# A gated delta rule in two halves of the tokens with all heads, and one attention pipeline over all head pairs

## The chip, the cores and the metric

The kernel runs on one core of a Trainium2 chip. The metric is the time of one execution on the device in microseconds; lower is better. The kernel before took 1449.81 us in the median of three runs (1449.51 to 1454.9).

## The reference

One transformer block in fp32: 1024 tokens, width 1024. The input is normalised and modulated by a condition vector (`mod`, six vectors of width 1024 from the product `silu(c) @ w_ada`), then projected. The projection feeds an attention with eight heads of 64 and a gated delta rule with eight heads of 64. Their outputs, side by side, pass an output projection `w_out`; a gated feed-forward network and a last normalisation follow.

```
proj = h @ w_in                      # q_a k_a v_a | q_d k_d v_d z_d | b_d a_d
y_attn  = dilated_attention(q_a, k_a, v_a, rel_bias)
qkv     = silu(causal_conv(q_d | k_d | v_d, width 4 along the tokens))
q, k    = l2norm per head;  beta = sigmoid(b_d);  g = -exp(a_log) * softplus(a_d + dt_bias)
# delta rule in chunks: within a chunk a unit lower triangular system is solved, then
for chunk in chunks:                 # one after the other, for each head
    v_new = u - w @ state
    o     = (q * exp(g)) @ state + qk @ v_new
    state = state * exp(g_last) + k_dec.T @ v_new
y_delta = rmsnorm(o) * silu(z_d)
x = x + g1 * (concat(y_attn, y_delta) @ w_out)
x = x + g2 * ((silu(h2 @ w_gate) * (h2 @ w_up)) @ w_down);  out = rmsnorm(x)
```

The outputs of a chunk depend on all earlier chunks of the same head through `state` alone; heads do not depend on each other.

## The kernel before

Engines are named as in the profile: PE (TensorE), DVE (VectorE), ACT (ScalarE), POOL (GpSimd), SP (which issues the DMAs). The kernel is one long program for a scheduler that puts the instructions into the queue of each engine. It follows program order as priority, by its own idea of when an operand is ready; an instruction that stands later in the program is moved ahead where it thinks an engine would be free. On the chip each engine works its queue in order.

**Products.** The large projections are done in two-part precision: each fp32 operand is split into a high and a low part, and three matmuls take the place of one. The split of the weights is `wsplit` (L209): a slab of 128 x 512 is loaded (256 KB, three buffers), cast on ACT (L215) and subtracted on POOL (L216), with five buffers for each part. The normalised input lies split in SBUF as `hh` and `hl`, eight tiles each.

**First stage (to about 113 us).** The first four column blocks (`first`: k and q of the delta heads 0 to 3) and two v blocks (L478, both halves of the tokens) are multiplied while the input is still being split (`normed`, `split`, L436 to L458). Two q blocks follow for the second token half (L602).

**Fill.** All other projections stand in a generator, `others` (L1103), that yields after every few matmuls with a nominal cost (0.64 us for three matmuls of 512 columns, 0.32 for three of 256). `proj_d` (L571) multiplies one block of 128 columns for both halves of the tokens with the same two slabs (10.24 nominal us); `proj_t` (L579) makes one block of 256 columns for all eight token blocks with four slabs (20.48). The order is: z of group 0; k, q and v of group 1; z of group 1; v of the attention (`va`, two blocks); q and k of the attention for the four head pairs. Results go to DRAM through `spill`. `mixed` (L1123) adds the modulation products (`mods`, L1081: a 256 KB load `wm` and eight small matmuls at a time). Fill is drawn at given points: `turn(name)` draws what `FILL[name]` says ahead of the product of that name and pins the product behind it, `until` draws until a part is done, and `hold(*LEVELS[g])` (L1136) draws until a part is done and then a stated number of nominal us, and pins the first step of the inverse behind it. FILL has 25 entries, `"trv3_0": 10.24` and `"S0_0_0": 14.08` the largest.

**Delta rule (about 95 to 482 us).** `delta(g)` (L1163) runs once for each of two groups of four heads, over all 1024 tokens: convolution (`conv`, L529), transposes (`delta_turn`, L705), decays and products within the chunk of 128 tokens (`delta_prep`, L730, kk at L776), v (`delta_v`, L821, transposes trv at L833), the inverse (`delta_inverse`, L843: 31 steps of substitution on DVE in blocks of 32, L862 and L866, a trip through DRAM, then the blocks joined per head) and the scan (`delta_scan`, L945). The scan takes the eight chunks in turn, each with two head pairs. A step of `state` (L946) is: two products with the state (L957), four operations R (L962), four products (L971), two copies, two products (L979) and four updates of the state S (L990). `readout` (L996) makes the output of the step before, `flip` (L1030) transposes it (yt, L1035) and stores it in DRAM. After the first scan `delta_early` (L1152) prepares q and k of group 1.

**Attention (482 to 711 us).** A unit is one head pair and one block of 128 queries: scores S (L1252, L1253), softmax, transposes tr (L1276, named et in FILL) and the product with the values y (L1293), pipelined over units in `attend` (L1308), the transposes one unit behind and the value products three behind:

```
    attend(range(EARLY))          # EARLY = 1: the eight units of pair 0
    run(fill[0])                  # all projections that are left
    sh_.close()                   # hh and hl are given up; yh, yl take their place
    ...                           # the delta rule's output is loaded (y_load)
    fill[0] = out_delta()         # half of the output projection is the new fill
    attend(range(EARLY, 4))       # the 24 units of pairs 1 to 3
```

`att_load` (L1205) loads q and k of a pair, head by head, into `raw` (two buffers) and converts them (QS, KS on ACT and DVE, KL on POOL). After this the rest of the output projection and the feed-forward network follow, which the change does not touch.

## Time and profile before

| | us |
|---|---|
| median of 3 runs | 1449.81 |
| lowest, highest run | 1449.51, 1454.9 |
| the profiled execution | 1446.69 |
| its span on the core | 1445.0 |
| mean granted clock of PE in it | 0.981 |

The span runs from the first to the last instruction; the execution's time has 1.7 us more around it. In the profile a group or a piece is named by line, engine, operation and output <- inputs, with shapes as partitions x elements and x for the number of instructions. A matmul's end is modelled, so that neighbouring matmuls overlap in the listing and a busy PE is not PE at its peak. The granted clock is a share of full speed.

### The profile page before, as it was taken

The numbers are of one execution on the slowest core, as the hardware profiler recorded it, in microseconds if no ns is written. First come the engines' busy times: TensorE is split into PE (matmuls) and PEld (weight loads), VectorE is DVE, ScalarE is ACT, GpSimd is POOL, SyncE is SP. The second block draws the span as 40 slices with busy tenths as digits, with TensorE's granted clock in tenths as the row PEclk, the third lists the DMA queues.
The fourth block names the chain that finished last, engine by engine and source line by source line (L and its number), as shares of the span: only waits on it lengthen the run. The fifth ranks groups of instructions, "written<-read, shape, count | busy, mean of one in ns | idle before, by whom it ended". The sixth has DMA issues, their size and how long they took to land.

```text
span 1445.0 us, 24561 instructions
## 1 busy us (share of the span) xinstructions
PE 1379.9 (95%) x8984; PEld 1119.5 (77%) x8984; DVE 873.4 (60%) x1660; ACT 670.0 (46%) x1283; POOL 305.2 (21%) x279
## 2 busy tenths in 40 slices
PE   7998989997999979999999989999999999999997
PEld 4777857786888758777877868888888888888885
DVE  3687762665736241366426997757676676475487
ACT  3487523348233263576437743333333333444456
POOL 1345412243323343444245310000000000000000
PEclk9998999998999989999999999999999999999999
DMA  8736464466532526642275445636354565866676
GB/s 304 246 114 175 136 200 144 147 191 178 158 95 63 172 68 182 189 132 92 81 237 167 154 138 173 206 111 210 125 178 144 167 211 182 268 213 206 191 222 236
DMA packets 171921, 245.69 MB, mean 170 GB/s; under 512 B 33078, under 2 KB 76391, under 8 KB 171800
## 3 DMA queue, kind: packets, MB, share of 16 engines
q1 hardware_dynamic: 171800, 244.12, 53.4%
q8 instruction: 71, 1.16, 0.3%
q14 instruction: 50, 0.41, 0.1%
HBM read 181.30 MB, written 67.48 MB: 172 GB/s over the span
## 4 chain that ended last, share of the span: by engine, by line
PE 62%; DVE 6%; DMA 5%; ACT 3%; issue 2%; POOL 1%; SPq 0%; DVEq 0%; ACTq 0%; POOLq 0%
PE wua L1525 8%; PE wga L1525 8%; PE X L1720 6%; PE g_a L567 5%; PE wuc L1525 4%; PE Z L1720 4%; PE wgc L1525 4%; PE g_va L590 4%; PE wo L567 2%; PE y L1293 2%; PE tr L1276 2%; PE Y L1720 2%; PE wgb L1525 2%; PE wub L1525 2%; PE S L1252 1%
## 5 line engine op out<-in xcount | busy, mean ns | idle before, releaser
L1515 DVE TENSOR_TENSOR wl_db<-wr_db,wh_db 128x512 fp32r<-128x512 f32 x77 | 53.2, 690 | 76.1 <-ACT wh_db L1514 75.9
L1514 ACT CAST wh_db<-wr_db 128x512 fp32r<-128x512 f32 x77 | 47.9, 622 | 98.3 <-PE X L1720 41.3
L1720 PE MATMUL X<-wl_db,wh_da 128*128 128x512 f32 x176 | 68.6, 390 | 0.2 <-DVE wl_db L1515 0.2
L1720 PE MATMUL X<-wh_db,wl_da 128*128 128x512 f32 x176 | 68.5, 389 | 0.0
L1720 PE MATMUL X<-wh_db,wh_da 128*128 128x512 f32 x176 | 68.5, 389 | 0.0
L1263 POOL TENSOR_SCALAR X<-X,sc 128x128 f32<-128x128 f32 (+7 forms) x64 | 47.8, 751 | 69.6 <-DVE sc L1262 57.2
L1261 ACT ACTIVATE X<-X,sc 128x128 f32<-128x128 f32 (+7 forms) x64 | 49.6, 776 | 22.8 <-DVE sc L1256 17.3
L1256 DVE CUSTOM_DVE_ANT_0 X<-S,ng 128x512 f32<-128x512 f32 (+3 forms) x64 | 36.9, 586 | 34.8 <-PE S L1253 25.8
L1515 DVE TENSOR_TENSOR wl_da<-wr_da,wh_da 128x512 fp32r<-128x512 f32 x77 | 52.7, 685 | 1.2 <-ACT wh_da L1514 1.2
L567 PE MATMUL wo<-yh,wh_wo 128*128 128x512 f32 x128 | 52.0, 408 | 0.7 <-ACT yh L1359 0.4
L567 PE MATMUL g_a<-hh,wh_a 128*128 128x512 f32 x128 | 51.4, 401 | 0.0
L567 PE MATMUL g_a<-hl,wh_a 128*128 128x512 f32 x128 | 51.1, 399 | 0.0
L567 PE MATMUL g_a<-hh,wl_a 128*128 128x512 f32 x128 | 51.0, 398 | 0.0
L567 PE MATMUL wo<-yl,wh_wo 128*128 128x512 f32 x128 | 50.6, 396 | 0.0
L567 PE MATMUL wo<-yh,wl_wo 128*128 128x512 f32 x128 | 50.5, 395 | 0.0
L1514 ACT CAST wh_da<-wr_da 128x512 fp32r<-128x512 f32 x77 | 47.3, 616 | 5.9 <-PE wua L1525 5.8
L1222 DVE SCALAR_TENSOR_TENSOR QS<-raw,QS 64x1024 fp32r<-64x1024 f32 x8 | 12.6, 1572 | 61.7 <-ACT QS L1221 61.6
L1276 PE MATMUL tr<-ident,X 128*128 128x128 f32 x288 | 45.2, 283 | 1.6 <-ACT et L1281 1.2
L1514 ACT CAST wh_wg_s<-wg_s 128x512 fp32r<-128x512 f32 x33 | 20.5, 622 | 55.4 <-PE wuc L1525 23.8
L1293 PE MATMUL y<-et,va 128*64 128x128 f32 x576 | 45.9, 285 | 0.0
L1252 PE MATMUL S<-KS,QS 128*128 128x512 f32 (+3 forms) x96 | 36.9, 394 | 7.3 <-ACT KS L1226 4.9
L216 POOL TENSOR_TENSOR wl_wo<-wr_wo,wh_wo 128x512 fp32r<-128x512 f32 x24 | 32.0, 1337 | 50.8 <-ACT wh_wo L215 40.7
(545 smaller groups left out, 4397.9 us busy)
## 6 DMA issues: line engine op xcount, KB each, us to landing
wr_da<-ao_d SPq DMA_DIRECT2D x77, 256.0 KB, 3.3
wm<-in_wada SPq DMA_DIRECT2D x64, 256.0 KB, 3.7
wr_wu<-in_wu SPq DMA_DIRECT2D x50, 256.0 KB, 2.8
wr_wg<-in_wg SPq DMA_DIRECT2D x48, 256.0 KB, 3.1
ao_d<-a SPq DMA_DIRECT2D x44, 256.0 KB, 2.6
wr_wd<-in_wdn SPq DMA_DIRECT2D x44, 256.0 KB, 3.1
wr_db<-wt_d SPq DMA_DIRECT2D x44, 256.0 KB, 2.9
ao_d<-as SPq DMA_DIRECT2D x33, 256.0 KB, 2.0
```

The lines of the kernel that those rows point to most:

```text
L567: last[0] = nc.tensor.matmul(ps, a[:, w0], b[k0 + k4][:, cs], start=(i == 0), stop=(i == n - 1))
L590: last[0] = nc.tensor.matmul(ps[:, :n], a[k][:, ts_], b[:, w0], start=(i == 0), stop=(i == 23))
L1252: nc.tensor.matmul(ps[:, 0 : c1 - c0], QS[:, qs], KS[:, c0:c1], start=True, stop=False)
L1256: nc.vector.tensor_tensor_reduce(out=X[:, c0:c1], in0=ps[:, 0 : c1 - c0], in1=ng[:, u + c0 : u + c1], scale=1.0, scalar=(3e38 if m is None ...
L1261: nc.scalar.activation(X[:, 0:nk], X[:, 0:nk], AF.Exp, scale=-1.0, bias=m, accum_out=sc[:, 2:3])
L1263: nc.gpsimd.tensor_scalar(out=X[:, 0:nk], in0=X[:, 0:nk], scalar1=sc[:, 3:4], scalar2=0.0, op0=ALU.mult, op1=ALU.add)
L1276: nc.tensor.transpose(ps[:, (kb - c0) * P : (kb - c0 + 1) * P], X[:, kb * P : kb * P + P], ident)
L1293: nc.tensor.matmul(yps[64 * e : 64 * e + 64, yc], va[:, kb, 64 * e : 64 * e + 64], ets[e][:, kb, :], start=(kb == 0), stop=(kb == qb),)
L1514: nc.scalar.copy(hi, src)
L1515: (eng or nc.vector).tensor_tensor(out=lo, in0=src, in1=hi.bitcast(F32), op=ALU.subtract)
L1525: nc.tensor.matmul(ps, a[:, w0], b, start=(first and k == 0 and n_ == 0), stop=(k == 3 and n_ == 2), skip_group_check=True,)
L1720: nc.tensor.matmul(bank[b], a[:, ts_], w, start=(first and f == 0 and n_ == 0), stop=(f == NF - 1 and n_ == 2), skip_group_check=True,)
```

## The change

The delta rule is cut the other way: `delta(g)` now runs over one half of the tokens (four chunks) for all eight heads, and the second run goes on from the state of the first. The scan has two times four steps with four head pairs each; the readout handles 512 columns at once.

- First stage: the four blocks of `first` are now k of all eight heads; the two blocks beside the input's split are q of pairs 0 and 1, for the first half of the tokens only; q of pairs 2 and 3 follows, first half only. v comes wholly from the fill, through DRAM.
- Fill: k, q, v and z are projected one half of the tokens at a time (`proj_h`, and `proj_t` over four token blocks), each time with slabs loaded anew. The order is v (first half), z (first half), k, q, v, z (second half), then va 0, pair 0, va 1, pair 1, pair 2, pair 3.
- Convolutions, transposes, norms and v are done on tiles of two pairs x 512 tokens. A convolution of the second half needs the last tokens of the first; they are kept as four columns ahead of it in DRAM.
- `LU`, the number of buffers of the tag that holds decays, v and the inverse, goes from 5 to 6. Small constants and the states move from one pool to another.
- `LEVELS` and `FILL` change: eight entries of FILL go, all of them for the delta rule.
- Attention: one pipeline over all 32 units. The fill that is left is dealt out evenly over the first 14 units (`FRONT` is the nominal sum of all fill), and the change of pools (`switch`) happens inside the pipeline, ahead of the value product of pair 1's fourth block. `raw` has four buffers instead of two.

```diff
-LEVELS = ("qd", 4), ("z1", 36)
+LU = 6
+LEVELS = (("qd", 1), 0), (("vd", 1), 24)
+FRONT = 4 * 20.48 + 4 * 5.12 + 5 * 10.24 + 8 * 10.24
...
-    "trv3_0": 10.24,
...
-    V0 = 16
+    V0 = 8
...
+    def proj_h(col, hf, name, evac):
+
+        slabs = [(wsplit(I["wd"][col, s], 512, f"{name}_{s}"), 4 * s) for s in range(2)]
+        ps = gbank(f"g_{name}")
+        yield from gemm(ps, slabs, hh, hl, slice(hf * HALF, (hf + 1) * HALF))
+        evac(hf, ps)
...
-        yield from proj_t(I["wz0"], 256, "z0", z_evac(0))
-        yield from group1(("kd", "qd", "vd"))
-        yield from proj_t(I["wz1"], 256, "z1", z_evac(1))
-        done.add("z1")
-        for c in range(2):
-            yield from proj_t(I["wva"][c], 256, f"va{c}", va_end(c))
-        done.add("va")
+        yield from half_of("vd", VD, range(4), 0)
+        for g in range(2):
+            yield from proj_t((I["wz0"], I["wz1"])[g], 256, f"z{g}_0", z_evac(g), range(4))
+        done.add(("z", 0))
+        yield from half_of("kd", KD, range(2, 4), 1)
+        yield from half_of("qd", QD, range(4), 1)
+        yield from half_of("vd", VD, range(4), 1)
+        for g in range(2):
+            yield from proj_t((I["wz0"], I["wz1"])[g], 256, f"z{g}_1", z_evac(g), range(4, 8))
+        done.add(("z", 1))
         for hp in range(4):
+            if hp < 2:
+                yield from proj_t(I["wva"][hp], 256, f"va{hp}", va_end(hp))
+                done.add(f"va{hp}")
...
             for Q in range(2):
+                with turn(f"sb{g}_{n}_{Q}"):
+                    for q in (2 * Q, 2 * Q + 1):
...
-        for n in range(8 + 3):
-            if n < 8:
+        for n in range(4 + 2):
+            if n < 4:
                 state(n)
...
-                r = pa.tile([P, T], F32, name=f"raw{kk}_{h}", tag="raw", bufs=2)
+                r = pa.tile([P, T], F32, name=f"raw{kk}_{h}", tag="raw", bufs=4)
...
-    def attend(hps):
-        units = [(hp, qb) for hp in hps for qb in range(TB)]
+    def attend(switch):
+        units = [(hp, qb) for hp in range(4) for qb in range(TB)]
         xs, ets = {}, {}
         for i in range(len(units) + AV):
+            if i >= AV and units[i - AV] == (EARLY, 3):
+                switch()
             if i < len(units):
                 hp, qb = units[i]
                 if hp not in loaded:
+                    until(lambda: hp in done)
                     loaded[hp] = att_load(hp)
-                if qb == 2 and hp < 3 and hp + 1 in done:
+                if i < EARLY * TB + 3 + AV:
+                    ahead((FRONT - used[0]) / (EARLY * TB + 3 + AV - i))
+                if qb >= 2 and hp < 3 and hp + 1 in done and hp + 1 not in loaded:
                     loaded[hp + 1] = att_load(hp + 1)
...
-    attend(range(EARLY))
-    run(fill[0])
-    sh_.close()
...
-    fill[0] = out_delta()
-    attend(range(EARLY, 4))
+    attend(switch)
```

More of the change, by code (lines that the diff above doesn't have):

```diff
@@ L482, in build @@
         for k in range(KT):
-            step(k, range(2))
+            if hf == 0:
+                step(k, range(2))
             split(k, hf)
@@ L800, in delta_prep @@
+        for q in range(4):
             with tc.issue_after(sel[g].ins):
@@ L953, in state @@
[L953 to L961 removed]
+            So = [S[q][N % 3] for q in range(4)]
+            Sn = [S[q][(N + 1) % 3] for q in range(4)]
@@ L1138, in hold @@
         until(lambda: what in done)
-        while us > 0:
-            us -= next(fill[0])
+        ahead(us)
         return tc.issue_after(last[0].ins)
@@ L1144, in until, with fetch @@
         while not ready():
-            next(fill[0])
-    def fetch(i, name):
-        xp = pd.tile([P, T], F32, name=f"xp_{name}", tag="xp", bufs=2)
-        nc.sync.dma_start(xp, _.pj[i])
+            used[0] += next(fill[0])
+    def fetch(i, hf, name):
+        xp = pd.tile([P, 2, XW], F32, name=f"xp_{name}", tag="xp", bufs=2)
+        c = (4, HALF)[hf]
+        for j in range(2):
+            nc.sync.dma_start(xp[:, j, c % HALF :], _.pj[i + j][:, c : HALF + 4 + HALF * hf])
         return xp
@@ L1859, in _layout @@
     qa, ka, va, qd, kd, vd, z, b, a = np.split(w, np.cumsum([512] * 7 + [8]), axis=1)
-    first = np.concatenate([kd[:, :256], qd[:, :256]], axis=1)
+    first = kd
+    pairs = [2 * q + e for e in range(2) for q in range(4)]
+    b, a = b[:, pairs], a[:, pairs]
     return {
```

492 lines of the change are left out of this document (255 added, 237 removed).

## The prediction

> **What bounds the kernel now.** I read the first page of the profile first, for the engine that carries the span.
>
> ```profile
> span 1445.0 us, 24561 instructions
> PE 1379.9 (95%) x8984; PEld 1119.5 (77%) x8984; DVE 873.4 (60%) x1660; ACT 670.0 (46%) x1283; POOL 305.2 (21%) x279
> PE 62%; DVE 6%; DMA 5%; ACT 3%; issue 2%; POOL 1%; SPq 0%; DVEq 0%; ACTq 0%; POOLq 0%
> ```
>
> TensorE (PE) is busy 95% of the span, so the span is PE's work plus the time in which PE has none. The regrouping changes no product of the computation (counts below), so what it can win or lose is PE's idle and badly used time between the first projections and the end of the attention, about 95 to 711 us. I cut that stretch by stage with the table of windows (start:end, length, busy us of PE, PEld, DVE, ACT, POOL with instruction counts, then the granted clock, the DMA share and GB/s):
>
> ```profile
> 95.00:240.00 145.00, 134.95 (x998) 104.55 (x999) 89.75 (x141) 73.68 (x136) 58.88 (x44) 0.94 0.57 167
> 240.00:482.00 242.00, 226.29 (x2436) 195.48 (x2430) 144.57 (x350) 100.61 (x224) 81.25 (x80) 0.97 0.44 131
> 482.00:508.00 26.00, 25.92 (x116) 21.34 (x116) 1.22 (x1) 7.88 (x14) 6.77 (x5) 1.00 0.68 202
> 508.00:552.00 44.00, 36.12 (x273) 27.69 (x272) 20.01 (x73) 24.19 (x56) 15.57 (x18) 0.88 0.24 72
> 552.00:603.00 51.00, 50.92 (x230) 41.66 (x226) 6.66 (x14) 20.95 (x43) 20.09 (x13) 1.00 0.72 203
> 603.00:711.00 108.00, 104.35 (x845) 81.20 (x844) 70.93 (x230) 72.59 (x161) 45.42 (x53) 0.98 0.34 103
> ```
>
> Rows one and two are the delta rule (two groups of four heads), row three the loading for the attention, row four the attention of head pair 0 alone, row five projections alone while VectorE (DVE) has 6.7 us of work, row six the attention of pairs 1 to 3. Row four stands out: PE has 7.9 us of nothing and a granted clock of 0.88, and right behind it come 51 us in which PE works and the others rest. Then I took the list of waits of PE, first for 95 to 482 us, then for the attention's start:
>
> ```profile
> PE mods L196 <- DVE mt L203: 4.3, 2, 3.9
> PE mods L196 <- DMA wm<-in_wada: 3.5, 3, 2.1
> PE trq_0False L714 <- ACT cv L536: 3.0, 1, 3.0
> PE kk_k L776 <- DVE qk L782: 3.0, 2, 2.6
> PE yt L1035 <- DVE o L1025: 2.4, 4, 1.2
> PE g_va L590 <- ACT va L1058: 2.1, 1, 2.1
> PE ps_GT L663 <- DVE Gc L655: 2.0, 1, 2.0
> PE ps_bp L757 <- DVE nbp L751: 1.5, 1, 1.5
> PE trv L833 <- ACT vd L536: 1.1, 1, 1.1
> PE g_qd L567 <- POOL hl L458: 0.9, 1, 0.9
> ```
>
> ```profile
> PE S L1252 <- ACT KS L1226: 4.9, 1, 4.9
> PE S L1253 <- POOL KL L1227: 2.3, 2, 1.2
> PE yt L1035 <- DVE o L1025: 1.3, 1, 1.3
> ```
>
> In the delta stages the waits sum to 23.8 us in single pieces of 1 to 4 us; none is a long stall behind the delta chain, because projections fill it. So halving the number of scan steps shortens a chain that PE mostly does not wait for.
>
> **Part 1: one attention pipeline (the main gain).** Before, pair 0's eight units run between 508 and 552 us, the pipeline drains, and the remaining projections run alone from 552 us. After, the projections that are left are dealt out evenly over the first 14 units. What pair 0's units cost PE now, by the groups of lines in the two windows (508 to 552, then 603 to 711), and the pace of a dense projection from the chain of waits:
>
> ```profile
> L567 PE MATMUL g_a<-hl,wh_a 128*128 128x512 f32 x4 | 2.0, 510 | 0.0
> L567 PE MATMUL g_a<-hh,wl_a 128*128 128x512 f32 x4 | 2.0, 511 | 0.0
> L567 PE MATMUL g_a<-hh,wh_a 128*128 128x512 f32 x3 | 1.8, 591 | 0.0
> L567 PE MATMUL wo<-yl,wh_wo 128*128 128x512 f32 x22 | 9.1, 415 | 0.0
> L567 PE MATMUL wo<-yh,wh_wo 128*128 128x512 f32 x21 | 9.0, 437 | 0.4 <-ACT yh L1359 0.4
> L567 PE MATMUL wo<-yh,wl_wo 128*128 128x512 f32 x22 | 8.5, 394 | 0.0
> 552.23 46.93 PE g_a L567 x206
> ```
>
> Dense, one matmul of 512 columns takes 46.93 / 206 = 0.228 us. Pair 0's eight units hold 11 of them: 44 - 11 x 0.228 = 41.5 us for the attention itself. Pairs 1 to 3 hold 65: 108 - 14.8 = 93.2 us for 24 units, 31.1 us for eight. The same work costs 10.4 us more in pair 0, where almost no projection stands between dependent steps and both heads' loads come late (the 4.9 and 2.3 us waits; `raw` goes from two to four buffers, so the second head's loads no longer wait for the first head's conversion). 10.4 us is the lower bound if the filled units reach the later pace. Upper bound: the first six units of pair 1, now filled too, cost 23.3 us at the later pace and could lose the same quarter, 5.8 us more, in all 16.2. I take **-14**, nearer the top because much more dense work stands between the steps: by the kernel's own costs four blocks of 20.48 us are left (one va block and pairs 1 to 3), some 5.9 us for each of the 14 units, where the later units now get 14.8 / 24 = 0.6. The loads of yd at the switch (8 DMAs, 8 ScalarE casts, 8 VectorE subtractions) now lie in the running pipeline; they did so at 603 us before. Covered by attention work they cost nothing, uncovered about 8 x 0.7 = 5 us on VectorE, which is idle 37 of 108 us there. SP's queue gets the same loads and spills, earlier.
>
> **Part 2: the scan, 2 x 4 steps with eight heads instead of 2 x 8 with four.** Products: 2 pairs x 7 steps x 2 groups = 28 state products become 4 pairs x 7 = 28; the readouts, the inverse (4 x 8 blocks per part), kk and the transposes keep their number too. VectorE in the first scan (262 to 306 us):
>
> ```profile
> L990 DVE SCALAR_TENSOR_TENSOR S<-S,eGl,st 64x64 f32<-64x64 f32 x24 | 6.7, 279 | 2.7 <-PE st L979 2.0
> L962 DVE SCALAR_TENSOR_TENSOR R<-st,nbg,vb 128x64 f32<-128x64 f32 x28 | 6.4, 278 | 1.9 <-PE st L957 1.7
> L1025 DVE TENSOR_TENSOR o<-o,zl 128x256 f32<-128x256 f32 x7 | 3.8, 540 | 0.1
> L1024 DVE TENSOR_TENSOR o<-o,of 128x256 f32<-128x256 f32 x8 | 3.4, 425 | 6.8 <-POOL of L1023 6.7
> ```
>
> A step has 4 + 4 of the small operations, 4 x 0.279 + 4 x 0.278 + 0.54 + 0.43 = 3.2 us; afterwards 8 + 8 and two operations of at most double length, 6.4 us. Half the steps at twice the work: the scan shortens only by its latency, from 44 to between 26 (4 x 6.4) and 44 us, and PE's own work in it stays. What PE gains is the waits that recur per step: yt, 2.4 + 1.3 = 3.7 us over 16 flips, half with 8: **-2** (0 to -3.7).
>
> **Part 3: the start.** 48 matmuls (the second token half of two v columns) leave the first stage and come back as fill, at nothing. The next product reads the first half of the tokens, so the 0.9 us wait on hl goes: **-1**.
>
> **Part 4: weights loaded once per half.** A half-width pass needs its slabs again: 14 half columns of kd, qd and vd replace six whole ones and the four slabs of two qd columns stay, so 16 slabs more; z is done twice, 8 more. Each of the 24 is a 256 KB load, a cast on ScalarE and a subtraction on GpSimd (POOL), by the groups of lines:
>
> ```profile
> L216 POOL TENSOR_TENSOR wl_z<-wr_z,wh_z 128x512 fp32r<-128x512 f32 x8 | 12.5, 1570 | 2.6 <-ACT wh_z L215 2.6
> L216 POOL TENSOR_TENSOR wl_qd<-wr_qd,wh_qd 128x512 fp32r<-128x512 f32 x7 | 10.3, 1479 | 40.3 <-ACT wh_qd L215 40.3
> ```
>
> 24 x 1.5 = 36 us on POOL, which is busy 58.9 of 145 us before 240. One slab now feeds 12 matmuls, 2.7 us of PE, instead of 24, 5.5 us; POOL makes one in 1.5 us. Bounds: 0 (the waits hold none on a slab's lower part) and 36 (all exposed). POOL's queue is in order, so a slab can stand behind `affine_select` waiting for its DMA, and all matmuls behind it. I take **+3**, near the lower bound by the row of waits, which has 0.9 us on POOL.
>
> [...] The first product of the substitution, in the first and in the second group, and POOL at the first:
>
> ```profile
> 169.69 1.10 DVE L862 TENSOR_TENSOR tm<-nt,tt 128x31 f32<-128x31 f32 x1
> 374.50 0.19 DVE L862 TENSOR_TENSOR tm<-nt,tt 128x31 f32<-128x31 f32 x1
> 168.54 4.70 POOL L216 TENSOR_TENSOR wl_kd<-wr_kd,wh_kd 128x512 fp32r<-128x512 f32 x3
> ```
>
> The same operation took 1.10 us beside a POOL subtraction and 0.19 us without one, 0.91 more. [...]
>
> **Part 5: the tuned paddings go.** FILL loses its delta entries, the large one 10.24 nominal us ahead of `trv3_0`. A yield of 0.64 is three matmuls, 0.68 us: 16 x 0.68 = 10.9 us of cover. Bounds: -1.1 (that wait goes, since with LU = 6 both v tiles exist at once) and +10.9. I take **+1**, near the lower bound: with five buffers the second v tile had to wait for the first one's transposes, which the sixth buffer ends, so less cover is wanted.
>
> **The sum.** -14 - 2 - 1 + 3 + 1 = -13. The profiled execution took 1446.7 us (1.7 us around its span), 3.1 below the median of 1449.8. On it 1433.7; on the median **1437**.
>
> **The rivals.**
> *No gain (0.15).* PE's 36.1 busy us in pair 0's window are real work, the fill merely lengthens its units: only the 7.9 idle us can go, parts 2 and 3 bring nothing, and parts 4 and 5 take 4: 1446, the same within the bound. For it: the modelled busy time. Against it: 41.5 against 31.1 us for equal work.
> *Slower (0.12).* Slabs starve PE: wherever POOL has over 2.7 - 1.5 = 1.2 us of other work per slab, PE waits, between 113 us and the inverse of the first half, when nearly all fill is half-width. All 24 exposed: 1449.8 - 17 + 36 + 1 = 1470. For it: POOL's share of 41% before 240 us rises by 12 to 16 slabs. Against it: no such wait now, five buffers ahead.
> *VectorE held up (0.08).* Every added subtraction stops a substitution step: 24 x 0.91 = 22 us on VectorE's chain, and PE's fill no longer covers it: 1449.8 - 17 + 22 + 1 = 1456. [...]
> *More (0.13).* The waits of the delta stages halve as well (-12): 1425.
> *My forecast (0.52).* 1437, its own range 1427 to 1446.
>
> **How the numbers follow.** What can be told from no change is about 0.5%, 7.2 us. Faster by more: 0.13, and 0.48 of the forecast's 0.52: 0.61. Within: 0.04 of it, 0.13 of "no gain", 0.02 of "VectorE": 0.19. Slower: the rest, 0.20, with 0.12 from starvation. The range runs from 1422 to 1460: it takes in "more", "no gain" and "VectorE", and leaves out the whole of the starvation case.
>
> **What would show it.** Right: no stretch of projections alone between two parts of the attention; S waits under 2 us in all at its start; the granted clock there at 0.97 or more; PE's waits from 95 us to the attention's start near 24 us; eight yt waits. Wrong: PE waiting on `wl` tiles of z, kd, qd or vd (starvation); substitution steps of over 1 us in the second half with the inverse's first product waiting (VectorE); pair 0's units without waits, and yet their attention part still near 41 us (no gain); a long PE wait on the v transposes of either half (part 5).

## The result, and the profile after

The changed kernel takes 1491.03 us in the median (1477.2 to 1504.35) against 1449.66 us of the kernel before on the same chip: a ratio of 1.0263, 95% interval 1.0223 to 1.0303. The ratio leaves out the longest of the four executions, 1504.35 us, which counts as slow because it is over 1.5% above the shortest. By the medians the changed kernel is 41 us slower; the forecast was 13 us faster, with a range to 1460. The profile is of that longest execution; its mean granted clock is 0.950 against 0.971 in the shortest, and its stretch of low clock has its own section below.

The first page of the profile after, the span, the busy times and the shares of the chain that ended last:

```profile
span 1502.6 us, 24656 instructions
...
PE 1412.3 (94%) x8984; PEld 1151.8 (77%) x8984; DVE 892.2 (59%) x1662; ACT 678.2 (45%) x1300; POOL 333.2 (22%) x301
...
PE 55%; DVE 5%; DMA 3%; issue 1%; ACT 1%; SPq 0%; DVEq 0%; ACTq 0%
```

PE has the same 8984 matmuls as before, yet 32 us more busy time: the same work at a lower mean clock, 0.950 against 0.981. And 1502.6 - 1412.3 = 90 us without work, where before had 65. The table of windows, cut by the stages of the changed kernel (start:end, length, busy us of PE, PEld, DVE, ACT, POOL with counts, granted clock, DMA share, GB/s):

```profile
95.00:254.00 159.00, 135.88 (x939) 103.04 (x939) 101.26 (x169) 80.99 (x162) 68.55 (x58) 0.91 0.64 183
254.00:432.00 178.00, 153.45 (x1478) 132.15 (x1476) 108.57 (x227) 73.48 (x150) 60.44 (x55) 0.86 0.49 148
432.00:485.00 53.00, 50.56 (x570) 45.00 (x571) 17.10 (x44) 14.23 (x33) 7.28 (x7) 0.52 0.23 61
485.00:547.00 62.00, 59.50 (x410) 54.15 (x409) 19.58 (x59) 15.03 (x31) 15.89 (x12) 0.97 0.47 132
547.00:603.00 56.00, 52.32 (x282) 44.10 (x283) 12.09 (x45) 25.29 (x59) 22.04 (x21) 0.94 0.41 111
603.00:770.00 167.00, 159.64 (x1203) 125.65 (x1203) 90.13 (x272) 99.36 (x215) 70.58 (x70) 1.00 0.40 117
```

In the attention (rows five and six) there is no stretch of projections alone, as forecast. Two other signs that the prediction named came short: the clock at its start is 0.94, not 0.97, and PE's waits at S come to 3.0 us between 547 and 603 us, not under 2. The loss lies ahead of the attention. Row three stands out: the inverse of the second half and the beginning of its scan run at a clock of 0.52 with PE nearly always busy. The list of waits of PE from 95 us to the attention's start:

```profile
PE trv L850 <- ACT vd L540: 16.6, 3, 13.1
PE mods L191 <- DVE mt L198: 8.7, 3, 4.7
PE ps_G L669 <- DVE t L666: 4.8, 1, 4.8
PE mods L191 <- DMA wm<-in_wada: 4.4, 2, 2.6
PE yt L1063 <- DVE o L1054: 4.3, 3, 2.3
PE lv L908 <- DMA tn<-tn_d: 4.0, 1, 4.0
PE trq_1False L737 <- ACT qd L540: 2.6, 1, 2.6
PE trk_2False L737 <- ACT kd L540: 2.2, 1, 2.2
PE mods L191 <- DVE mods L1115: 2.2, 1, 2.2
```

Before, no wait in this stretch was over 3.9 us, and together they were 23.8. Now the third v transposes of the second half alone wait 13.1 us. There is still no row for a lower part `wl` of a slab.

**A common measure for all runs.** Fill moves between stages from kernel to kernel, so stage lengths cannot be compared directly. I take the length of each stage and subtract the projections that lie in it, at their full-clock pace: 0.228 us for 512 columns (from the prediction), and for 256 columns the distance of two starts in PE's timeline, 0.12 us:

```profile
429.92 0.28 PE L603 MATMUL g_va<-wl_va,hh 128*128 128x256 f32 x1
430.04 0.28 PE L603 MATMUL g_va<-wh_va,hh 128*128 128x256 f32 x1
```

What is left is the stage's own work with its idle time and its low clock. Stages by first matmuls: (a) up to the first transposes of k; (b) to the first inverse (`lv`); (c) to the last `yt` of the first scan; (d) to the second inverse; (e) to the attention's first S; (f) to the first product of the feed-forward network. In us, from the profiled execution of each kernel:

| kernel | a | b | c | d | e | f | median, us |
|---|---|---|---|---|---|---|---|
| before | 102.2 | 53.5 | 52.8 | 46.7 | 45.6 | 239.0 | 1449.66 |
| after | 97.1 | 67.8 | 55.2 | 63.9 | 70.3 | 233.2 | 1491.03 |
| after, two attends (e3) | 97.3 | 64.3 | 54.6 | 59.9 | 63.8 | 237.1 | 1491.35 |
| after, padding ahead of trv (e1) | 97.3 | 67.9 | 54.1 | 55.5 | 50.5 | 232.0 | 1479.25 |
| after, v first (e5) | 97.1 | 66.8 | 54.9 | 55.4 | 51.1 | 234.3 | 1475.81 |
| after, v and decay loads early (e16) | 97.2 | 64.8 | 47.5 | 52.7 | 52.2 | 234.7 | 1471.45 |
| after, 18 slabs fewer (e14) | 98.6 | 60.2 | 50.9 | 54.6 | 52.3 | 232.0 | 1466.06 |
| before, 24 slabs more (e7) | 102.0 | 69.7 | 58.8 | 50.5 | 48.1 | 241.0 | 1475.31 |
| before, 24 loads more (e11) | 101.7 | 55.7 | 54.9 | 54.5 | 45.6 | 239.7 | 1457.71 |
| before, 24 splits more (e13) | 99.4 | 58.5 | 52.8 | 49.9 | 47.3 | 241.0 | 1456.76 |
| before, one pipeline (e2) | 100.8 | 54.4 | 53.9 | 43.5 | 45.6 | 236.6 | 1443.55 |

In column a the changed kernels have 48 matmuls, 10.9 us, less to do, so 97.1 there is 5.8 us worse than before, not 5.1 better. The row "after" against "before": +5.8, +14.3, +2.4, +17.2, +24.7, -5.8, in all 58.6, which is the difference of the two spans (57.6) within a microsecond.

### The profile page after: what moved, and what is told of

Same layout as the page of the kernel before. It is cut to its first block, busy times and chain, and to the rows that moved or that the text cites. A ratio compares the mean times of both kernels' runs of the same rounds, so it can differ in the third digit from the quotient of the medians.

```text
span 1502.6 us, 24656 instructions
## 1 busy us (share of the span) xinstructions
PE 1412.3 (94%) x8984; PEld 1151.8 (77%) x8984; DVE 892.2 (59%) x1662; ACT 678.2 (45%) x1300; POOL 333.2 (22%) x301
## 4 chain that ended last, share of the span: by engine, by line
PE 55%; DVE 5%; DMA 3%; issue 1%; ACT 1%; SPq 0%; DVEq 0%; ACTq 0%
PE wua L1572 8%; PE wga L1572 7%; PE X L1767 7%; PE g_a L573 5%; PE wo L573 5%; PE Z L1767 4%; PE wuc L1572 4%; PE wgc L1572 4%; PE Y L1767 2%; PE y L1331 2%; PE wgb L1572 2%; PE wub L1572 2%; PE tr L1314 2%; PE S L1290 1%; PE S L1291 1%
## 5 line engine op out<-in xcount | busy, mean ns | idle before, releaser
L1301 POOL TENSOR_SCALAR X<-X,sc 128x128 f32<-128x128 f32 (+7 forms) x64 | 49.9, 782 | 83.7 <-DVE sc L1300 82.0
L1562 DVE TENSOR_TENSOR wl_da<-wr_da,wh_da 128x512 fp32r<-128x512 f32 x77 | 52.7, 685 | 1.2 <-ACT wh_da L1561 1.2
L573 PE MATMUL wo<-yl,wh_wo 128*128 128x512 f32 x128 | 50.5, 394 | 1.4 <-DVE yl L1393 1.4
L1561 ACT CAST wh_da<-wr_da 128x512 fp32r<-128x512 f32 x77 | 47.3, 616 | 5.9 <-PE wua L1572 5.8
L191 PE MATMUL mods<-wm,cc 128*32 128x128 f32 x512 | 33.8, 309 | 15.3 <-DVE mt L198 8.7
L1561 ACT CAST wh_wg_s<-wg_s 128x512 fp32r<-128x512 f32 x33 | 20.5, 622 | 55.5 <-PE wuc L1572 23.9
L1331 PE MATMUL y<-et,va 128*64 128x128 f32 x576 | 42.8, 279 | 0.1
L1314 PEld LDWEIGHTS tr<-ident,X 128*128 128x128 f32 x288 | 32.9, 140 | 12.0 <-issue 4.7
```

The costliest lines, as they stand in the source:

```text
L191: nc.tensor.matmul(ps[32 * j : 32 * j + 32, 0 : 32 * nt], win, v[:, j], start=False, stop=last, skip_group_check=True)
L573: last[0] = nc.tensor.matmul(ps, a[:, w0], b[k0 + k4][:, cs], start=(i == 0), stop=(i == n - 1))
L1301: nc.gpsimd.tensor_scalar(out=X[:, 0:nk], in0=X[:, 0:nk], scalar1=sc[:, 3:4], scalar2=0.0, op0=ALU.mult, op1=ALU.add)
L1314: nc.tensor.transpose(ps[:, (kb - c0) * P : (kb - c0 + 1) * P], X[:, kb * P : kb * P + P], ident)
L1331: nc.tensor.matmul(yps[64 * e : 64 * e + 64, yc], va[:, kb, 64 * e : 64 * e + 64], ets[e][:, kb, :], start=(kb == 0), stop=(kb == qb),)
L1561: nc.scalar.copy(hi, src)
```

## The experiments

Each stands as a short diff, with what was expected of it on record. Ratios are against the kernel before, with 95% intervals.

**The parts of the change by themselves: pipeline and paddings**

e2, the kernel before with the one pipeline (FRONT drawn evenly over the first 14 units, four raw buffers):

```
-    attend(range(EARLY))
-    run(fill[0])
...
-    attend(range(EARLY, 4))
+    attend(switch)
```

> The kernel before with the one attention pipeline alone (part 1 of the prediction): one attend over all 32 units, fill dealt evenly over the first 14, four raw buffers, the delta rule untouched. The prediction's part 1: -14 (between -10.4 and -16.2), 1436. Theory from the comparison of the two traces (the attention's stretch of the changed kernel is only 5.6 us better than before when its additional matmuls are taken off): -4 to -7, 1443 to 1446, with waits on sc, et and QS in place of the long ones on KS and KL. No effect: 1450.

Measured: 1443.55 us, ratio 0.9965 (0.9943 to 0.9987): 5.1 us faster, a third of the -14. The gain is small, but its interval lies below 1; this version beats both kernels.

e3, the changed kernel with the two attends of before (the same diff backwards).

> The kernel after with part 1 undone: two attends, the fill run out between them, two raw buffers. If the pipeline is worth 5 us in the changed kernel too: 5 us slower than after, 1496. If it is worth 14: 1505. If the one pipeline costs time there (fill drawn early, so that the dense work stands where the clock is already full): 1485 or less.

Measured: 1491.35 us, 1.0260 (1.0206 to 1.0314), the same as after. Its attention, column f, is 3.9 us longer, but column e, with its low clock, is 6.5 us shorter, so the medians cannot show what the pipeline is worth here.

e4, the kernel before without the delta entries of FILL:

```
-    "sy1_6": 1.92,
-    "kk1_3_0_k": 0.64,
-    "trv3_0": 10.24,
...
```

> The kernel before without the delta entries of FILL that the change removes (trv3_0 with 10.24 and seven of 0.64 or 1.92), all else as before: part 5 alone. The prediction's part 5: +1 (between -1.1 and +10.9), 1451. Theory A (a missing padding costs the stall and then the clock behind it): a wait of about 10 us on the v transposes of group 1, a granted clock near 0.5 in the products behind it, and 15 to 30 us more, 1465 to 1480. Theory B (the paddings matter little, since the fetch of v is not late in the kernel before): within 3 us of 1450.

Measured: 1447.76 us, 0.9986 (0.9967 to 1.0006): nothing, as theory B has it. The paddings were not needed even with the old structure.

**The slabs**

e7, the kernel before, each of 24 slabs loaded and split again for the second half of the tokens:

```
         for hf in range(2):
+            if hf == 0 or name[0] != "a" or name[-1] == "0":
+                slabs = [(wsplit(...), 4 * s) for s in range(2)]
...
+            if tb == 4 and name[0] == "z":
+                slabs = [wsplit(src[s], 2 * n, f"{name}b_{s}") for s in range(4)]
```

> The kernel before with 24 slabs loaded and split a second time for the second half of the tokens (k, q and v of the second group, both z blocks, q and k of the first attention pair), no other change: part 4 of the prediction alone, which took +3 (0 to 36). Theory A (slabs are hidden): within 4 us of before, 1448 to 1452. Theory B (slabs starve PE or stop VectorE, and carry much of the loss): 1460 to 1485, with PE waits on wl tiles or substitution steps of over 1 us.

Measured: 1475.31 us, 1.0167 (1.0135 to 1.0199), 24 us more: theory B in its amount, a good half of the whole loss, without any of the regrouping. But theory B's signs came hardly or not at all: substitution steps of over 1 us are 14 of 124, where the kernel before has 10, and waits on `wl` are missing. PE's waits between 95 and 250 us in this kernel:

```profile
PE mods L196 <- DVE mt L203: 7.9, 3, 5.9
PE mods L196 <- DMA wm<-in_wada: 7.7, 8, 2.1
PE ps_bp L760 <- DVE nbp L754: 2.4, 1, 2.4
...
PE g_qd L567 <- ACT sp_kd L1070: 1.6, 1, 1.6
```

No `wl` at all. The cost is paid by other work: in the same window the kernel before had 4.3 on mt (the row stands in the prediction), 2.7 on wm, and no wait on nbp or sp_kd.

```profile
PE mods L196 <- DMA wm<-in_wada: 2.7, 2, 2.1
```

The four rows are 12.6 us more, most of the 16.2 of column b. What the queues do, by the groups of lines between 95 and 255 us (busy, mean ns, then the idle time before them and who ended it), first ACT's casts before, then with the slabs:

```profile
L215 ACT CAST wh_qd<-wr_qd 128x512 fp32r<-128x512 f32 x7 | 4.2, 615 | 9.9 <-PE g_kd L567 5.2 <-issue 2.4 <-DMA wr_qd<-in_wd 2.3
```

```profile
L215 ACT CAST wh_qd<-wr_qd 128x512 fp32r<-128x512 f32 x11 | 6.7, 615 | 28.1 <-PE g_kd L567 19.1 <-PE g_qd L567 5.2 <-issue 3.8
```

The casts wait for buffers that PE has not freed, 19.1 us on g_kd alone, and what stands behind them on ACT waits too. ACT works its queue in order: in after two z products, the last matmul of which starts at 377.06 us, are copied out only from 393.45, behind v's convolution, which waits 8.6 us for its load. That suggested the ring of five buffers. e9, the same with eight:

```
-        hi = wp.tile(..., tag="wh", bufs=5)
-        lo = wp.tile(..., tag="wl", bufs=5)
+        hi = wp.tile(..., tag="wh", bufs=8)
+        lo = wp.tile(..., tag="wl", bufs=8)
```

> The kernel before with 24 slabs loaded and split twice (as in the run that does this alone, 25 us slower than before), now with eight buffers instead of five for each part of a slab. Theory A (the cost is the ring: a slab feeds half as much PE work, the casts wait in ACT's in-order queue for a buffer that PE has not freed, and everything behind them on ACT and then PE waits): most of the 25 us goes, 1450 to 1460. Theory B (the cost is the work of the slabs itself on ACT, GpSimd and the DMA queues): it stays, 1468 to 1478.

Measured: 1470.51 us, 1.0129 (1.0083 to 1.0175), inside theory B's span; its interval overlaps that of e7. The casts wait no less (23.5 us on g_kd for the same group). The ring is not the main cause; that it has a small part is not excluded.

e11 repeats only the loads, into the raw buffers; e13 only 24 casts on ACT and 24 operations on POOL into the ring, with the same values:

```
+    def again(src, name):
+        raw = wp.tile([P, slot], F32, name=f"wr2_{name}", tag="wr", bufs=3)
+        nc.sync.dma_start(raw, src)
```

```
+            nc.scalar.copy(hi, slab[0].bitcast(F32))
+            nc.gpsimd.tensor_tensor(out=lo, in0=slab[1].bitcast(F32), in1=nul, op=ALU.add)
```

> The kernel before with the same 24 slabs loaded a second time, but neither cast nor subtracted (the first parts are used for both halves): the DMA and SP's queue alone. If the loads carry the cost (SP's queue waits for a raw buffer, the mods weights behind it come late): 1460 or more, with waits on wm. If the split carries it: within 4 us of before, 1447 to 1454.

> The kernel before with 24 additional casts on ACT and 24 additional operations on GpSimd into the same ring of five buffers (copies of both parts of a slab, with the same values), no additional load: ACT, GpSimd and the ring alone. Theory A and B of the slabs both expect most of the 25 us here, 1464 to 1478; if the loads carry it: 1447 to 1455.

Measured: 1457.71 us, 1.0066 (1.0041 to 1.0091), and 1456.76 us, 1.0061 (1.0039 to 1.0083). Neither carries it: loads alone 9.6 us, splitting alone 8.8, both together 24.2 (the ratios on 1447.77 and 1450.02). The loads cost in column d (+7.8), the splits in b (+5.0) and d (+3.2). Both together cost 5.8 us more than the sum of the two. The half widths of the three intervals are 4.6, 3.6 and 3.2 us, so it is not shown that they do more together than apart.

e14, in the changed kernel: the ten half columns of k, q and v of the second half all use the slabs of the first of them, so that 18 slabs are left out and the result is not the reference's:

```
+                if hf == 1 and not held:
+                    held.extend((wsplit(...), 4 * s) for s in range(2))
```

> The kernel after, but the ten half columns of k, q and v of the second token half are all multiplied with the two slabs of the first of them (so these projections have other weights than the reference): 18 of the additional slabs are neither loaded nor split, PE's work is the same. Theory A (slabs cost about 1 us each here too, as the 24 did in the kernel before): 14 to 22 us less than after, 1469 to 1477, or about 1460 where the granted clock stays up ahead of the second inverse. Theory B (in the changed kernel the stall at v and the clock are all of the loss, and the slabs cost nothing beside them): within 5 us of after, 1486 to 1496.

Measured: 1466.06 us, 1.0124 (1.0076 to 1.0173), 25 us less than after. Part of that is the clock: column e is 18.0 us shorter than in after. Without that column the other five stages are 20.9 us shorter than in after: 1.2 us a slab, 28 us for the 24. Beside e5, which had the clock too but projects v earlier, the sum over all stages is 11.0 us less: 0.6 us a slab, 15 us for the 24. Each figure comes of one execution a kernel; between 15 and 28 us is what they tell.

**The stall on v, and where it went**

The third v transposes wait for ACT, and ACT waits for the load of v. The timeline of SP's queue around it:

```profile
374.81 0.60 SPq L1096 DMA_DIRECT2D pj_d<-sp_vd  x1
...
383.62 0.33 SPq L209 DMA_DIRECT2D wr_va<-in_wva  x1
384.00 0.43 SPq L1096 DMA_DIRECT2D pj_d<-sp_vd  x1
384.47 0.42 SPq L1183 DMA_DIRECT2D xp_v<-pj_d  x1
...
387.05 0.32 SPq L1183 DMA_DIRECT2D xp_v<-pj_d  x1
```

The fetch is issued at 384.47, right behind the spill of the same block, and that stood behind a slab load which waited for its buffer. That load is only the last of what held it. ACT had copied the block out by 338.41 us, and the three longest waits of SP's queue between 336 and 385 us are these:

```profile
337.77 0.64 ACT L1095 COPY sp_vd<-g_vd 128x256 f32<-128x256 f32 x2
```

```profile
SPq L1119 <- PE mods L191: 10.1, 7, 2.1
SPq L803 <- DVE dt L799: 8.8, 4, 2.6
SPq L209 <- POOL wl_va L211: 2.7, 1, 2.7
```

The loads for the modulation products wait for buffers that PE frees, the stores of the decay products wait for DVE, and the spill and the fetch stand in order behind both. Four ways to free it were tried. e1 puts padding ahead of the transposes; e5 projects v of the second half before k and q; e8 adds to e5 that the fetch has priority on SP's queue; e15 leaves the order and issues spill and fetch from POOL's queue:

```
+    "trv1_2": 20.48,                                         # e1
```

```
+        yield from half_of("vd", VD, range(4), 1)            # e5, ahead of kd and qd
```

```
+            with urgent() if name[:3] == "v1_" else ...:     # e8, on top of e5
```

```
-            nc.sync.dma_start(xp[:, j, ...], ...)            # e15
+            (nc.gpsimd if name[:3] == "v1_" else nc.sync).dma_start(xp[:, j, ...], ...)
```

> The kernel after with one more entry in FILL: 20.48 nominal us of projections ahead of the third v transposes of the second half (trv1_2), so that PE has work while the fetch of that v pair, its convolution and its silu come in. Theory A (a stall of PE there, and the lower granted clock in the thin work behind it, carry most of the loss of 41 us): the wait of 13.1 us on vd goes, the granted clock of 430 to 490 us returns to 0.9 or more instead of 0.50, and the time falls by 25 to 40 us, to 1451 to 1466. Theory B (the loss is spread: twice the slabs, VectorE held up, a slower first stage): the 13 us appear again as another wait a little later (the transposes wait for the same DMA), the clock stays low, and the time falls by 0 to 5 us, to 1486 to 1491.

> The kernel after with the fill in another order: the second token half of v is projected before that of k and q, not behind it, with the same number of products ahead of the first inverse (LEVELS names kd instead of qd). Theory A (the stall on the third v transposes is the late spill and fetch of v: the fetch stood on SP's queue behind a spill that stood behind decay loads, lt_d stores and slab loads): the 13.1 us wait on vd falls to under 4 us, PE's idle time between the last yt of the first scan and the first lv of the second inverse falls from 22.5 to about 12 us, and the time to 1470 to 1480. Theory B (the fetch is late for another reason: its buffer, or the convolution in the queues of ACT and VectorE): the wait stays over 8 us, 1485 to 1495.

> The same reordered kernel, with the fetch of v for the second half also put ahead on SP's queue (issued with the priority that slab loads have). If SP's order is all of it: no wait on vd above 2 us, and 2 to 6 us less than with the reordering alone. If the reordering has freed the fetch already: the same within 3 us. If the early fetch blocks SP's queue for others: waits on DMA grow, up to 10 us more.

> The kernel after with the stores of v of the second token half, and the loads that bring it back, issued on GpSimd's queue instead of SP's; nothing else moves. Theory A (the 13.1 us stall on the third v transposes is SP's in-order queue, in which these stand behind stores that wait for decay products): that wait falls under 4 us and PE's idle time between the first scan and the second inverse from 22.5 to 10 to 14 us; the time falls by 8 to 20 us. Theory B (the chain of the second half's preparation is late as a whole, so that the wait moves to the decay loads, the buffers of z or to tn): the idle time stays above 18 us and the time within 6 us of after.

Measured: e1 1479.25 us, 1.0208 (1.0175 to 1.0241); e5 1475.81, 1.0198 (1.0151 to 1.0245); e8 1481.46, 1.0234 (1.0180 to 1.0288); e15 1484.98, 1.0235 (1.0187 to 1.0284). In e1, e5 and e15 the long wait on v goes and another takes its place, in e5 this one, in e1 the same with 10.7 and in e15 with 8.5:

```profile
PE g_z L603 <- ACT zt L629: 9.9, 1, 9.9
```

The bank of a z product is not emptied, since ACT stands in order behind v's convolution and the decay loads `eb`. In e8 no single wait is over 5.8 us, but many are left (8.2 us on v in three pieces, 5.8 on tn), and its column d is no shorter, 56.5. So e16: e8, with the `eb` loads ahead on SP's queue too.

```
+                  with urgent() if g else ExitStack():
                     nc.sync.dma_start(eb[64 * e : 64 * e + 64, i], ...)
```

> The kernel after with v of the second half projected first (as in the run with that alone), and with both the fetch of v and the decay loads eb of the second half put ahead on SP's queue. In the runs so far the wait on v only moved: to the buffers of z, 8.5 to 10.8 us, while ACT's queue stood still for eb and for v's convolution. Theory A (SP's in-order queue is the whole of it, once eb is freed too): no single wait over 4 us between the first scan and the second inverse, PE's idle time there 8 to 13 us instead of 22.5, the time 1462 to 1470. Theory B (the preparation chain of the second half is longer than the fill that stands there, whatever the order on SP): idle time 17 us or more there, the time 1474 to 1485.

Measured: 1471.45 us, 1.0132 (1.0093 to 1.0171), the best of the changed kernels that do the whole computation, but again with the wait moved on, now to q, whose load stands behind those put ahead of it:

```profile
PE kk_q L793 <- DMA qd<-cv_d: 12.0, 1, 12.0
PE lv L909 <- DMA tn<-tn_d: 6.7, 1, 6.7
```

By idle time theory B holds: PE is idle for 21.0 us between the first scan and the second inverse, 22.1 in after. The time lies between the two theories. Whichever load is put first, the waits move more than they go. Column d is 52.7 to 63.9 in all changed kernels but the next, against 46.7 before. In which order on SP the whole preparation would come in time was not found.

e17, e16 with the 18 slabs of e14 left out:

> The same, and the ten half columns of k, q and v of the second half multiplied with the two slabs of the first of them (other weights than the reference; 18 slabs fewer, PE's work the same). If slabs and the late preparation are the two parts of the loss and add up: 10 to 14 us less than the run beside it, 1450 to 1458 under theory A, 1462 to 1472 under theory B.

Measured: 1461.0 once and 1488.3 to 1498.1 three times, so there is no ratio. The 1461.0 lies between the two theories; the profile is of one of the others, with the low clock, 72.7 us in column e and 50.7 in d.

**The low clock**

In the profile after, the thin products of the second inverse (32 x 32 and 64 x 64) run at half clock. Two windows inside it, after and e1:

```profile
437.00:470.00 33.00, 33.00 (x427) 29.48 (x425) 10.62 (x23) 9.90 (x23) 5.13 (x6) 0.50 0.16 49
```

```profile
437.00:455.00 18.00, 17.82 (x398) 14.21 (x398) 8.98 (x19) 8.05 (x20) 4.50 (x5) 1.00 0.18 53
```

In after PE has no idle time at all for 33 us, and the clock stays at 0.50; in e1 nearly as many matmuls take 18 us at 1.00. Sixteen of them in a row, after and then e1 (start, length of all):

```profile
441.50 1.97 PE L937 MATMUL lw<-tc,dt 64*64 64x64 f32 x16
```

```profile
438.77 1.14 PE L938 MATMUL lw<-tc,dt 64*64 64x64 f32 x16
```

Column e has two levels: 45.6 to 52.9 with the clock, 63.8 to 72.7 without. From 90 us to the first S, e1 has 56.6 us without work and after 53.2 (sums of 5 us windows), so the 12 us between their medians are not idle time; by column e they are the clock. What sets it off? e6 lengthens the fill ahead of the second inverse, to remove the 4.0 us wait on tn; e12 and e18 shorten it in the kernel before, to make such a wait:

```
-LEVELS = (("qd", 1), 0), (("vd", 1), 24)
+LEVELS = (("qd", 1), 0), (("vd", 1), 40)        # e6, on the kernel after
```

```
-LEVELS = ("qd", 4), ("z1", 36)
+LEVELS = ("qd", 4), ("z1", 28)                  # e12, on the kernel before; 24 in e18
```

> The kernel after with 40 instead of 24 nominal us of fill between the substitution of the second half and its inverse, all else as it is: the v stall of 13 us stays, and the wait of 4.0 us on tn ahead of the thin products of the inverse goes. Theory A (the low granted clock of 0.50 from 440 to 480 us is set off by that small wait, ahead of thin products that never bring the clock back): the clock there is 0.95 or more, 10 to 20 us less than after, about 1475. Theory B (the low clock comes of the thin products themselves, or of the long stall before): 0.5 to 0.7 in that stretch again, and within 5 us of after, 1486 to 1496.

> The kernel before with 28 instead of 36 nominal us of fill between the substitution of the second group and its inverse. It takes 8.5 us of cover away. [...] Theory B (the wait costs itself): 0 to 8 us, 1450 to 1458, the clock back after 5 to 10 us.

> The kernel before with 24 instead of 36 nominal us of fill ahead of the inverse of the second group (28 made it 4 us slower, with a wait of 3.5 us on tn; of its ten runs two took 1469). Now the wait should be 6 to 8 us. Theory A (the length of the stall ahead of the thin products decides: beyond about 4 us the granted clock stays at 0.5 through the inverse and the scan, as it did in the changed kernel behind waits of 4.0 and 5.8 us): most runs at 1465 to 1475, the clock at 0.50 for 30 us or more behind the wait. Theory B (the two runs of 1469 had nothing to do with it): 1453 to 1460 with the clock back within 10 us.

Measured: e6 1490.31 us, 1.0271 (1.0204 to 1.0337): the wait on tn went, a wait of 3.9 us on the bank of va came 4 us ahead of the same products, and the clock fell all the same. e12 1451.97 us, 1.0049 (1.0011 to 1.0087), e18 1453.14 us, 1.0027 (1.0005 to 1.0048). Both have the same fill there, and the waits came out alike, 3.5 and 3.2 us, not the 6 to 8 that I had expected of e18. But the two profiles differ, e12 first:

```profile
435.00:470.00 35.00, 32.37 (x264) 30.37 (x261) 23.52 (x81) 11.76 (x35) 15.84 (x17) 1.00 0.27 77
```

```profile
435.00:470.00 35.00, 35.00 (x318) 32.18 (x315) 9.62 (x26) 6.54 (x17) 3.53 (x4) 0.50 0.03 9
```

e18's profile is of an execution of 1473.45 us, with 67.1 us in column e, e12's of one of 1451.46 with 48.6. Of the 23 runs of both kernels four are at 1468.8 to 1475.0, the others at 1445.5 to 1458.7; of the four, only the one of 1473.45 has a profile. Of 91 runs of the kernel before, none is over 1458.8. Of e4, whose profile shows no such gap, one of 12 is at 1473.4, and what held that one is not known. So such a gap (3.5 us in e12, 3.2 in e18) ahead of the thin products seems to make the low clock possible in the kernel before as well, but not certain. Its length does not decide: e16 had the clock back 6.8 us after it fell, behind a gap of 6.7 us. What does is open. Theory A of e18 is right about the place and the price, some 20 us, and wrong that the length of the gap decides.

The traces hold one candidate. In before and after all changes of the granted clock lie whole multiples of 3.41 us apart, as if on a grid: in after it is 0.50 from 433.81 to 485.01 us, 15 times 3.41, in before from 413.93 to 417.34, once. The low stretches of e16, e17 and e18 at this inverse, by their 5 us windows, are 6.8, 54.6 and 51.2 us long, 2, 16 and 15 times 3.41. In ten profiles the inverse follows the gap directly. In the five that stayed low a line of this grid falls within 0.7 us of the inverse's first product (0.6 in after, 0.2 in e17, 0.4 in e18); in the five that had the clock back the nearest is 1.1 to 1.6 us away (1.4 in e16). This was read off afterwards and not tested, and e6, where other products stand between gap and inverse, does not fit it.

**A version meant to beat both**

e10, e2 with seven buffers for each slab part (bufs=7 in place of 5 for `wh` and `wl`):

> The kernel before with the one attention pipeline and seven instead of five buffers for each part of a slab, nothing of the regrouped delta rule. If more buffers help the casts of the kernel before too: 3 to 6 us less than with the pipeline alone, 1437 to 1441; if the ring is no limit there: as the pipeline alone, 0.35% less than before, 1442 to 1445.

Measured: 1445.59 us, 0.9964 (0.9929 to 1.0000): as the pipeline alone. By the medians e2 stays the fastest.

## Why the prediction was wrong, by its steps

**Part 4 is the term that failed.** It took +3 between 0 and 36, "near the lower bound by the row of waits, which has 0.9 us on POOL". Alone in the kernel before it is 24 us (e7), in the changed one 15 to 28 by e14. The row was read for the wrong thing. It says whether PE waits for a slab; it does not say whether PE waits for what stands behind slabs on ACT, SP and POOL. The remark that "a slab can stand behind `affine_select`" looked in one direction only: what stands behind a slab was not asked. The sign named for starvation, waits on `wl`, came to no more than one wait of 0.8 us in three of the kernels, though the 24 us of e7 are nearer to starvation's price of 36 than to my 3. With 24 in place of 3 the sum is +8: the sign of the forecast turns, and 1458 is still inside the range. What carries the kernel out of the range is in the parts below.

VectorE was a smaller matter. That every added subtraction costs a substitution step 0.91 us, which gave the rival "VectorE held up" its 22 us, no run shows. The first substitution between 95 and 260 us, before and then with the 24 slabs:

```profile
L862 DVE TENSOR_TENSOR tm<-nt,tt 128x31 f32<-128x31 f32 (+15 forms) x31 | 14.5, 468 | 1.1
L866 DVE TENSOR_TENSOR tt<-tt,tm 128x31 f32<-128x31 f32 (+15 forms) x31 | 13.2, 425 | 1.0
```

```profile
L865 DVE TENSOR_TENSOR tm<-nt,tt 128x31 f32<-128x31 f32 (+15 forms) x31 | 16.5, 533 | 1.1
L869 DVE TENSOR_TENSOR tt<-tt,tm 128x31 f32<-128x31 f32 (+15 forms) x31 | 15.1, 487 | 1.0
```

It takes 3.9 us more in 62 operations, about a sixth of the 22, and the second substitution is as long as before (25.9 against 25.7 us). The subtractions are the likely cause: with the loads alone (e11) the first substitution takes 28.1 us against 27.7 before, with the splits alone (e13) 32.9.

**Part 1, -14, had its size wrong.** It measured -5.1 (-8.3 to -1.9), less than its own lower bound of 10.4. The wait of 4.9 us on KS went, as said, but in e2 one of 5.2 us took its place, a projection whose bank the spill had not emptied:

```profile
PE g_a L570 <- ACT sp_a L1070: 5.2, 1, 5.2
```

Column f is 2.4 us shorter in e2 and 5.8 in after, not 10.4 or more. So most of what pair 0's units cost above later ones does not go when they are filled, as the rival "no gain" held. The step that failed is the lower bound: that filled units reach the pace of the later ones.

**Part 2, -2,** was taken from the yt waits, and these did not go: 4.3 us in 3 pieces, 3.7 in 5 before. The first scan itself (column c) is 5.3 us shorter in e16, where the clock is 1.00 through it as in the kernel before, and 2.4 longer in after, where it is 0.90. So the first scan is shorter only where the clock holds; of the second nothing is left, since column e is 50.5 to 52.9 with the clock against 45.6 before.

**Part 3, -1, had the wrong sign.** The wait on hl went from 0.9 to 0.7, but PE waits 4.8 us on ps_G, the first decay product, in every changed kernel, and column a loses 5.8 us. I read it so that the 48 matmuls taken out of the first stage had covered the chain to that product; no run puts them back, so this is not shown. "At nothing" named no cover for what stayed behind.

**Part 5, +1:** the paddings are worth nothing (e4). Yet the sign that I had attached to it, a long wait on the v transposes, was the largest new wait. Its cause is the second half's preparation, whose spills, decay loads and fetches share SP's queue in a new order: the +6 to +17 us of column d. No term of the sum had it: the prediction says only that "SP's queue gets the same loads and spills, earlier", and that of the attention.

**The clock** was not a term either. The some 20 us of column e come in some executions and not in others: of the four of the changed kernel one takes 1477.2, with a mean granted clock of 0.971, and three 1490 to 1504, with 0.950 to 0.961.

For a run with the clock the stages of e5 give the account: +5.8 first stage, +13.3 slabs and preparation of the first half, +2.1 scan, +8.7 preparation and +5.5 inverse and scan of the second half, -4.7 attention, in all +30.7, where the spans differ by 30.1. Column b, on which the prediction put 3 us, is the largest of them, but without it the sum would still be +17.4: the slabs do not explain the loss alone.

## What to carry to other kernels

A weight that is loaded and prepared once more cost more here than its waits on PE show (24 us in e7, with no wait on `wl`): price it on every in-order queue that it passes, by what stands behind it, and test it alone: one run of the old kernel with nothing but the slabs loaded and split again (e7) would have turned this forecast's sign. The loads without the splits (9.6 us, e11) would not have. When fill is taken out of a stage, look for the chain that it covered there, even if the fill comes back elsewhere. A gap of 3.2 to 6.7 us ahead of the thin products was followed in six profiles by a stretch at half clock that cost some 20 us, so keep such a gap away from them; in e6 the 4 us of dense products that stood between gap and inverse were not enough.

## What the runs showed of the hardware

In six executions (after, e3, e6, e8, e17, e18; mean granted clock 0.950 to 0.961) the granted clock did not come back while PE was busy with the products of the second inverse; in after PE was busy for 33.00 of 33.00 us at 0.50. It came back 3 to 13 us after the last 64 x 64 product, when the scan's 128 x 128 products had begun (after: the last one ends at 472, the clock is 1.00 from 485; e18: 461 and 470; e3: 464 and about 468). Twelve profiles have a gap of 3.2 to 6.7 us ahead of this inverse, in ten of them just ahead. In eleven the clock falls behind it; in the kernel before it falls behind less, at 413.9 us after 3.9 us in which PE was idle for 2.1:

```profile
410.00:413.90 3.90, 1.79 (x15) 1.58 (x14) 1.74 (x4) 3.00 (x8) 0.00 (x0) 1.00 0.20 69
413.90:417.30 3.40, 3.40 (x17) 3.40 (x18) 0.00 (x0) 0.08 (x1) 0.00 (x0) 0.50 0.22 77
```

In six of the eleven it stays at half to the inverse's end; in e16 it was back 6.8 us after it fell, in after 51.2 us.

At half clock the 64 x 64 products take nearly twice as long: sixteen in a row 1.97 us (after) in place of 1.14 (e1). The length of a single one in the profile, 311 ns in place of 218, hides this, since a matmul's end is modelled; two neighbours start 107 ns apart in place of 58.
